# Three feed-forward layers by seven products instead of eight in 31 inner blocks, with one buffer pool and some low parts made by DMA

## The chip, the cores and the metric

The kernel runs on one core of one Trainium2 chip. The metric is the device time of one execution in microseconds (us).

## What is computed

Two layers of a diffusion trunk over 256 latent tokens (`L`) and 256 context tokens (`C`), 1024 features each. Every layer is a half-step SwiGLU feed forward, a token mixer (retention in layer 0, 2-D neighbourhood attention in layer 1), and another half-step feed forward; each is preceded by an RMS norm and a shift and scale taken from a modulation vector (`SiLU(c)` times a large matrix).

```python
def swiglu(x, w_in, w_out):
    a, b = jnp.split(x @ w_in, 2, axis=-1)
    return (jax.nn.silu(a) * b) @ w_out
# x: 256 + 256 tokens x 1024, w_in: 1024 x 5632, w_out: 2816 x 1024, four times
```

The fourth feed forward only has the latent tokens.

## The kernel before

Everything is kept in single precision on TensorE by splitting each operand into a high part (a rounding copy to the `float32r` format, made by ScalarE) and a low part (operand minus high part, made by VectorE). A product is then three matmuls: high weight by high input, high weight by low input, low weight by high input (`acc3`, L614). Every matmul is issued at L259, every VectorE, ScalarE and GpSimd operation at L151, every load at L166, so the rows are told apart by tile names: `raw` (a weight as loaded), `whi` and `wlo` (its parts), `slot` (activations and their parts), `t` (scratch), `pair` and `one` (PSUM: two banks, or one bank, of 512 words per partition), `acc` and `mraw` (the modulation).

A feed forward has 22 inner units of 128 hidden features. For one unit (`ffn`, the loop over `t`), two outputs of 128 features (a and b) are accumulated over eight blocks of 128 inputs, three matmuls each, with all 512 tokens as columns: 48 matmuls, the two outputs in the two banks of a `pair`. `gated_part` (L750) then makes silu(a) on ScalarE, the product on VectorE, and its high and low part. After 11 inner units the eight output blocks of `wout` are accumulated over those 11, and `residual` (L853) adds each to the stream `h`; then the other 11 units and eight blocks follow. In the last two output blocks the two streams are done apart, 256 columns at a time, so that the next norm can start.

The order is written by a planner: each emitted instruction advances an estimated clock of its engine (`account`, L131, with a fixed cost and a rate for each engine), and `advance` (L228), called after every matmul, emits pending VectorE and ScalarE steps when their estimated time has come. Steps wait in lists: `later` (evacuations, through `at`), `soon` (weight parts), and `bg`, the modulation of later sublayers, which VectorE computes by multiply-adds of 128x512 in the background, one step each `BG_EVERY` us of planned TensorE time. `mcol` (L445) hands out modulation columns that must be there by then. Weights are loaded in the order of `plan`: two raw buffers, three buffers for each part. Each engine executes its instructions in the order in which they were emitted; buffers and PSUM banks are guarded by semaphores.

## Time and profile before

| | |
|---|---|
| runs | 1949.91, 1951.44, 1952.09 us, median 1951.44 |
| the profiled execution | 1952.25 us, of which the span from first to last instruction is 1950.2 us |
| TensorE clock granted, mean | 0.994 of full speed |
| HBM | 276.11 MB read, 142 GB/s over the span |
| inner units of the three feed forwards with both streams | 66, at 48 matmuls of 512 columns |

Busy times of an engine are sums of its instructions' records. Matmuls are pipelined, so a matmul's recorded duration is longer than its distance to the next one, and a TensorE that is busy all the time can still be made to do less work. The distance from start to start is what one matmul costs in a dense stretch.

### The profile page before, as it was taken

The numbers are of one execution on the slowest core, as the hardware profiler recorded it, in microseconds if no ns is written. First come the engines' busy times: TensorE is split into PE (matmuls) and PEld (weight loads), VectorE is DVE, ScalarE is ACT, GpSimd is POOL, SyncE is SP. The second block draws the span as 40 slices with busy tenths as digits, with TensorE's granted clock in tenths as the row PEclk, the third lists the DMA queues.
The fourth block names the chain that finished last, engine by engine and source line by source line (L and its number), as shares of the span: only waits on it lengthen the run. The fifth ranks groups of instructions, "written<-read, shape, count | busy, mean of one in ns | idle before, by whom it ended". The sixth has DMA issues, their size and how long they took to land.

```text
span 1950.2 us, 26148 instructions
## 1 busy us (share of the span) xinstructions
PE 1924.2 (99%) x10458; PEld 1661.8 (85%) x10458; DVE 1352.0 (69%) x2402; ACT 687.9 (35%) x1035; POOL 73.0 (4%) x108
## 2 busy tenths in 40 slices
PE   7999999999999999999999999999999999999998
PEld 4888888898888888888888889888888899989998
DVE  5576666678788888876666676767632588887665
ACT  5422232333323232342222223322222366665443
POOL 1000000010000000100000000000000101100000
PEclk8999999999999999999999999999999999999999
DMA  7334534434434434234353343555433345544553
GB/s 287 141 137 129 187 130 136 156 119 151 142 133 141 147 130 142 86 130 149 125 179 132 140 139 98 194 189 200 162 101 82 110 119 113 98 115 167 194 176 114
DMA packets 70090, 278.85 MB, mean 143 GB/s; under 512 B 23632, under 2 KB 23888, under 8 KB 52304
## 3 DMA queue, kind: packets, MB, share of 16 engines
q1 hardware_dynamic: 69968, 277.18, 43.5%
q8 instruction: 82, 1.34, 0.3%
q14 instruction: 40, 0.33, 0.0%
HBM read 276.11 MB, written 1.05 MB: 142 GB/s over the span
## 4 chain that ended last, share of the span: by engine, by line
PE 94%; DVE 3%; ACT 2%; DMA 1%; issue 0%; SPq 0%; DVEq 0%; ACTq 0%
PE pair L259 61%; PE one L259 32%; DVE slot L151 1%; PE one L265 1%; DMA slot<-in_wmod 1%; DVE t L151 1%; ACT slot L151 1%; DVE wlo L151 1%; ACT whi L151 1%; DVE few L151 0%; DMA raw<-in_nv 0%; ACT t L151 0%; DVE h L151 0%; PE pair L265 0%; SPq L166 0%
## 5 line engine op out<-in xcount | busy, mean ns | idle before, releaser
L259 PE MATMUL pair<-slot,whi 128*128 128x512 f32 (+2 forms) x4000 | 1039.1, 351 | 6.8 <-ACT slot L151 4.7
L259 PEld LDWEIGHTS pair<-slot,whi 128*128 128x128 f32 x4000 | 696.4, 190 | 104.3 <-ACT slot L151 5.4
L259 PE MATMUL pair<-slot,wlo 128*128 128x512 f32 (+2 forms) x2000 | 682.5, 350 | 0.1
L259 PE MATMUL one<-slot,whi 128*128 128x512 f32 (+1 forms) x1860 | 481.4, 347 | 0.0
L151 DVE TENSOR_TENSOR wlo<-raw,whi 128x1024 fp32r<-128x1024 f32 (+1 forms) x400 | 436.4, 1122 | 38.5 <-ACT whi L151 37.7
L151 ACT CAST whi<-raw 128x1024 fp32r<-128x1024 f32 (+1 forms) x400 | 365.0, 959 | 225.3 <-PE one L259 138.6
L259 PEld LDWEIGHTS pair<-slot,wlo 128*128 128x128 f32 x2000 | 372.9, 190 | 48.8 <-DVE wlo L151 0.4
L259 PEld LDWEIGHTS one<-slot,whi 128*128 128x128 f32 x1860 | 325.9, 189 | 43.4
L259 PE MATMUL one<-slot,wlo 128*128 128x512 f32 (+1 forms) x930 | 323.1, 347 | 0.0
L151 DVE SCALAR_TENSOR_TENSOR acc<-mraw,sT,acc 128x512 f32<-128x512 f32 x392 | 279.2, 750 | 17.1 <-DMA mraw<-in_wmod 15.9
L151 ACT ACTIVATE t<-pair 128x512 f32<-128x512 f32 x66 | 39.4, 597 | 442.9 <-PE pair L259 442.9
L259 PEld LDWEIGHTS one<-slot,wlo 128*128 128x128 f32 x930 | 176.1, 189 | 21.8
L151 DVE TENSOR_TENSOR t<-pair,t 128x512 f32<-128x512 f32 x66 | 45.6, 692 | 204.2 <-ACT t L151 204.2
L151 DVE TENSOR_TENSOR slot<-t,slot 128x512 fp32r<-128x512 f32 (+2 forms) x144 | 88.1, 612 | 64.8 <-ACT slot L151 63.4
L151 ACT CAST slot<-t 128x512 fp32r<-128x512 f32 (+2 forms) x144 | 79.4, 552 | 122.1 <-DVE t L151 121.7
L151 DVE SCALAR_TENSOR_TENSOR h<-one,gate,h 128x256 f32<-128x256 f32 x112 | 49.6, 479 | 103.6 <-PE one L259 103.4
L151 POOL TENSOR_TENSOR t<-t,t 128x256 f32<-128x256 f32 x47 | 39.4, 850 | 1708.4 <-ACT t L151 1286.9
L259 PE MATMUL pair<-whi,slot 128*128 128x512 f32 (+1 forms) x384 | 98.5, 339 | 0.0
L259 PE MATMUL one<-slot,slot 128*128 128x512 f32 (+1 forms) x432 | 89.8, 348 | 1.3 <-DVE slot L151 1.0
L151 ACT ACTIVATE t<-h 128x256 f32<-128x256 f32 (+1 forms) x88 | 36.9, 434 | 142.8 <-DVE h L151 129.3
L259 PEld LDWEIGHTS one<-slot,slot 128*128 128x128 f32 x432 | 69.9, 189 | 10.8 <-DVE slot L151 1.4
L259 PEld LDWEIGHTS pair<-whi,slot 128*128 128x128 f32 x384 | 67.2, 189 | 7.5
(100 smaller groups left out, 1077.8 us busy)
## 6 DMA issues: line engine op xcount, KB each, us to landing
raw<-in_win SPq DMA_DIRECT2D x88, 1024.0 KB, 4.9
mraw<-in_wmod SPq DMA_DIRECT2D x128, 512.0 KB, 4.7
raw<-in_wout SPq DMA_DIRECT2D x64, 704.0 KB, 4.2
slot<-in_wmod SPq DMA_DIRECT2D x16, 512.0 KB, 10.3
raw<-in_rv SPq DMA_DIRECT2D x8, 1024.0 KB, 4.8
raw<-in_rg SPq DMA_DIRECT2D x8, 1024.0 KB, 4.9
raw<-in_ro SPq DMA_DIRECT2D x8, 1024.0 KB, 4.9
slot<-in_ex SPq DMA_DIRECT2D x8, 512.0 KB, 6.0
```

The lines of the kernel that those rows point to most:

```text
L151: getattr(self.real, op)(*args, **kw)
L259: nc.tensor.matmul(out, lhsT=lhsT, rhs=rhs, start=start, stop=stop)
L265: nc.tensor.transpose(out=out, in_=in_, identity=ident)
```

## The change

In 31 of the 66 units (7, 12 and 12 of the three feed forwards: `STANDARD` gives the first unit, `AMONG` the pattern) the product is arranged as a 2 by 2 block product: two outputs (a, b), two halves of the inputs (four blocks of 128 each), two token streams. Eight block products are replaced by seven with sums (Strassen's scheme in Winograd's form). Each of the seven has 4 blocks by 3 matmuls of 256 columns (`product`). The sums of the weight blocks are made on VectorE (`Seven`), the sums of the input blocks once for each feed forward (`operands`, not shown below: eight sums of 128x512 and four of 128x1024, and four pairs of parts of 128x1024), and the sums of the results when PSUM is read (`seven`). The low part of the b block of each such unit is not subtracted by VectorE: ScalarE writes minus the high part, and a DMA from GpSimd's queue reads the weight again from memory and adds it (`low_by_dma`). The same is done to half of every weight of the two mixers (`mixed`, 48 weights). Further: one pool of 40 buffers of 4 KB takes the place of three pools with the same room in all; weights are loaded in pieces of 512 KB; the 22 units are cut into three parts (8, 7, 7) in place of two, in all four feed forwards; the planner's fixed costs and rates are other ones; `BG_EVERY` is 0.9; a modulation column that isn't made when it is asked for is made there and then.

```diff
-HALF = NHC // 2
+PARTS = ((0, 8), (8, 15), (15, 22))
...
+SLOTS, RAWS, SPLITS = 40, 4, 12
+DMA_LOW = True
+MIXED = True
 BIG = 1e30
+STANDARD, AMONG = (8, 5, 5), (2, 3, 3)
...
-    slots = ctx.enter_context(tc.tile_pool(name="slots", bufs=24))
+    slots = ctx.enter_context(tc.tile_pool(name="slots", bufs=SLOTS))
...
-    V = Engine("dve", nc.vector, 0.06, 960.0)
-    A_ = Engine("act", nc.scalar, 0.09, 1200.0)
+    V = Engine("dve", nc.vector, 0.157, 960.0)
+    A_ = Engine("act", nc.scalar, 0.155, 1150.0)
...
+    def in_seven(f, t):
+        return f < 3 and t >= STANDARD[f] and (t - STANDARD[f]) % AMONG[f] < AMONG[f] - 1
+    def halves(src):
+        k = src.shape[1] // 2
+        return [src[:, i * k:(i + 1) * k, :] for i in range(2)]
+    def plan_ffn(f):
+        for p, (t0, t1) in enumerate(PARTS):
+            for t in range(t0, t1):
+                if in_seven(f, t):
+                    plan.append(("seven", [a["wrow"][f, t, r] for r in range(2)]))
+                else:
+                    plan.append(("plain", halves(a["win"][f, t])))
+            plan.extend(("plain", [a["wout"][f, n][:, t0:t1, :]]) for n in range(KC))
...
+        two = lambda *srcs: plan.extend((MIXED and "mixed" or "plain", halves(x)) for x in srcs)
...
-        account("pe", [lhsT, rhs], [out], n / 2400.0 * (1 if rhs.dtype == F32R and n >= 256 else 4) + 0.0025)
+        account("pe", [lhsT, rhs], [out], n / 2400.0 * (1 if rhs.dtype == F32R and n >= 256 else 4) + 0.0136)
...
+    def low_by_dma(lo, hi, src):
+        A_.activation(out=lo, in_=hi.bitcast(F32), func=AF.Copy, scale=-1.0)
+        nc.gpsimd.dma_start(out=lo.rearrange("p (k c) -> p k c", k=src.shape[1]), in_=src.bitcast(F32R), accum_op=ALU.add)
+        now["dma"] = max(now["dma"], now["act"])
+        account("dma", [], [lo], P * int(np.prod(src.shape[1:])) * 4 / 190e3)
+        ready[key(lo)] = (now["dma"] + 4.0, "dma")
...
+            if kind == "mixed" and i == 1:
+                def second(hi=hi, lo=lo, src=src, n=n):
+                    low_by_dma(lo[:, :n], hi[:, :n], src)
...
+            def low_b():
+                lo, hi = part_tile(), self.tiles["b", 0]
+                self.tiles["b", 1] = lo
+                low_by_dma(lo, hi, srcs[1])
...
+            steps = [(0.0, cast("b", rb), rb, 1), (0.8, DMA_LOW and low_b or low("b", rb), rb, 1), (1.5, p1, ra, 0),
+                     (2.2, p1_hi, ra, 1), (2.4, add(ra[:, f0], ra[:, f0], rb[:, f0]), ra, 0),
+                     (3.2, add(rb[:, f0], lambda: box["p1"], rb[:, f0]), rb, 0), (4.0, p1_lo, rb, 0),
+                     (4.6, add(rb[:, f1], rb[:, f0], rb[:, f1]), rb, 0), (5.2, cast("p", rb), rb, 1),
+                     (6.0, low("p", rb, True), rb, 1), (7.0, cast("a", ra), ra, 1), (8.0, low("a", ra, True), ra, 1)]
...
+            tile, last, half = {"b0": ("b", 1, 0), "b1": ("b", 1, 1), "p1": ("p1", 6, None), "a1": ("a", 11, 1),
+                                "p3": ("a", 11, 0), "p2": ("p", 9, 0), "p4": ("p", 9, 1)}[name]
+            force(self.no, last)
+            return [(t if half is None else t[:, half * 512:half * 512 + 512]).rearrange("p (k c) -> p k c", k=4)
+                    for t in (self.tiles[tile, 0], self.tiles[tile, 1])]
...
+    def released(n):
+        state["parts"] -= n
+        pump()
...
-            if raws and state["split"] - state["retired"] < SPLITS:
+            if raws and (not split_tiles if raws[0][0] == "seven" else
+                         state["parts"] + 2 * len(raws[0][1]) <= state["limit"] and not any(x[6] for x in soon)):
...
-    BG_EVERY = 2.2
+    BG_EVERY = 0.9
...
-        assert all((l, v, (c0 + k) // 4) in made for k in range(kk.start, kk.stop))
+        while not all((l, v, (c0 + k) // 4) in made for k in range(kk.start, kk.stop)):
+            if due:
+                mod_sum(*due.pop(0)[1])
+            else:
+                next(bg, None)
...
+    def product(w, name, x7, out):
+        wh, wl = w.part(name)
+        for k in range(4):
+            xh, xl = x7[name](k)
+            mm(out, lhsT=wh[:, k, :], rhs=xh, start=k == 0, stop=False)
+            mm(out, lhsT=wh[:, k, :], rhs=xl, start=False, stop=False)
+            mm(out, lhsT=wl[:, k, :], rhs=xh, start=False, stop=k == 3)
+    def seven(t, dst, x7):
+        w = weight()
+        p, b_, u_, a_, m1 = pair(), t512(), t512(), t512(), t256()
+        both = lambda x: x.rearrange("p (s t) -> p s t", t=S)
+        twice = lambda x: x.unsqueeze(1).broadcast_to([P, 2, S])
+        then = lambda step, on=None, us=0.2: at(us, L, t, step, on)
+        product(w, "b0", x7, p[:, 0, 0:S])
+        then(lambda: A_.copy(out=m1, in_=p[:, 0, 0:S]))
+        product(w, "b1", x7, p[:, 1, 0:S])
+        released(2)
+        product(w, "p2", x7, p[:, 1, S:T2])
+        then(lambda: V.tensor_tensor(out=both(b_), in0=both(p[:, 1, :]), in1=twice(m1), op=ALU.add))
+        q = pair()
+        product(w, "p3", x7, q[:, 1, S:T2])
+        product(w, "p1", x7, q[:, 1, 0:S])
+        released(1)
+        then(lambda: V.tensor_tensor(out=both(u_), in0=both(q[:, 1, :]), in1=twice(b_[:, S:T2]), op=ALU.add))
+        product(w, "p4", x7, q[:, 0, S:T2])
+        released(2)
+        then(lambda: V.tensor_tensor(out=b_[:, S:T2], in0=q[:, 0, S:T2], in1=u_[:, 0:S], op=ALU.add))
+        product(w, "a1", x7, q[:, 0, 0:S])
+        released(2)
+        then(lambda: V.tensor_tensor(out=both(a_), in0=q[:, :, 0:S], in1=twice(u_[:, S:T2]), op=ALU.add))
+        then(lambda: A_.activation(out=a_, in_=a_, func=AF.Silu, scale=-1.0), a_, 0.0)
+        then(lambda: V.tensor_tensor(out=b_, in0=b_, in1=a_, op=ALU.mult), a_, 0.0)
+        then(lambda: A_.copy(out=dst[:, 0, :], in_=b_), b_, 0.0)
+        then(lambda: V.tensor_tensor(out=dst[:, 1, :], in0=b_, in1=dst[:, 0, :].bitcast(F32), op=ALU.subtract), dst, 0.0)
...
-            for t in range(len(gts), HALF):
+            for t in range(len(gts), size):
+                if t0 + t == standard:
+                    x7 = made_operands()
+                    state["limit"] = SPLITS
+                if in_seven(2 * l + which, t0 + t):
+                    gts.append(slot([P, 2, 512], F32R))
+                    seven(t, gts[t], x7)
+                    continue
+                if not raw and t0 + t == standard - 3 and standard < PARTS[0][1]:
+                    made_operands = operands(xt)
+                if t0 + t == standard - 3 and standard == PARTS[0][1]:
+                    state["limit"] = SPLITS - 4
...
+            if raw or t1 > standard:
+                need(L, size - 2)
             for w, ps in zip(ws, pss):
-                acc3_part(ps[:, every], terms(w, every, range(HALF - 1)), True, False)
-            if raw:
-                need(L, HALF - 1)
+                acc3_part(ps[:, every], terms(w, every, range(size - 1)), True, False)
+            if raw or t1 > standard:
```

## Rows read from the trace of the kernel before

**Rows 1.** The page's first part: engine, busy us (share), instructions.

```profile
PE 1924.2 (99%) x10458; PEld 1661.8 (85%) x10458; DVE 1352.0 (69%) x2402; ACT 687.9 (35%) x1035; POOL 73.0 (4%) x108
```

**Rows 2.** The page's chain that ended last, by engine.

```profile
PE 94%; DVE 3%; ACT 2%; DMA 1%; issue 0%; SPq 0%; DVEq 0%; ACTq 0%
```

**Rows 3.** Windows: stretch, us, then busy us and count of each engine, clock, DMA.

```profile
175.00:295.00 120.00, 120.00 (x533) 99.38 (x532) 80.67 (x131) 28.82 (x36) 0.00 (x0) 1.00 0.45 155
...
440.00:835.00 395.00, 393.95 (x1927) 333.15 (x1926) 327.75 (x605) 128.67 (x171) 7.49 (x10) 1.00 0.39 132
...
1560.00:1755.00 195.00, 189.97 (x1383) 177.70 (x1384) 163.36 (x331) 124.56 (x231) 25.00 (x32) 1.00 0.51 111
```

**Rows 4.** Timeline of an inner unit, 512 columns: start, us, engine, operation.

```profile
1033.55 0.62 PE L259 MATMUL pair<-slot,whi 128*128 128x512 f32 x2
...
1043.78 0.62 PE L259 MATMUL pair<-slot,whi 128*128 128x512 f32 x2
```

**Rows 5.** Timeline of the last output blocks, 256 columns.

```profile
1175.53 0.40 PE L259 MATMUL one<-slot,whi 128*128 128x256 f32 x2
...
1184.89 0.40 PE L259 MATMUL one<-slot,whi 128*128 128x256 f32 x2
```

**Rows 6.** Groups by form, VectorE: out, in, count, busy us, mean ns.

```profile
L151 DVE TENSOR_TENSOR wlo<-raw,whi 128x1024 fp32r<-128x1024 f32 x272 | 324.3, 1222 | 21.5 <-ACT whi L151 21.0
L151 DVE SCALAR_TENSOR_TENSOR acc<-mraw,sT,acc 128x512 f32<-128x512 f32 x392 | 279.2, 750 | 17.1 <-DMA mraw<-in_wmod 15.9
L151 DVE TENSOR_TENSOR wlo<-raw,whi 128x704 fp32r<-128x704 f32 x128 | 112.1, 910 | 17.1 <-ACT whi L151 16.7
L151 DVE TENSOR_TENSOR slot<-t,slot 128x512 fp32r<-128x512 f32 x98 | 67.8, 692 | 56.8 <-ACT slot L151 56.3
L151 DVE SCALAR_TENSOR_TENSOR h<-one,gate,h 128x256 f32<-128x256 f32 x112 | 49.6, 479 | 103.6 <-PE one L259 103.4
...
L151 DVE TENSOR_TENSOR t<-one,t 64x256 f32<-64x256 f32 x16 | 6.7, 420 | 0.6 <-ACT t L151 0.2
L151 DVE TENSOR_TENSOR t<-t,t 128x512 f32<-128x512 f32 x8 | 5.5, 693 | 0.3
```

**Rows 7.** Groups by form, ScalarE.

```profile
L151 ACT CAST whi<-raw 128x1024 fp32r<-128x1024 f32 x272 | 272.0, 1045 | 117.7 <-PE one L259 102.2 <-DMA raw<-in_win 7.2 <-issue 4.7
...
L151 ACT CAST slot<-t 128x512 fp32r<-128x512 f32 x98 | 60.8, 621 | 96.1 <-DVE t L151 96.0
...
L151 ACT ACTIVATE t<-pair 128x512 f32<-128x512 f32 x66 | 39.4, 597 | 442.9 <-PE pair L259 442.9
...
L151 ACT COPY slot<-one 128x256 f32<-128x256 f32 x1 | 0.4, 373 | 5.9 <-PE one L259 5.9
```

**Rows 8.** DMA queues and issues: KB each, median us to landing.

```profile
q1 hardware_dynamic: 69968, 277.18, 43.5%
...
mraw<-in_wmod SPq DMA_DIRECT2D x128, 512.0 KB, 4.7
...
slot<-in_wmod SPq DMA_DIRECT2D x16, 512.0 KB, 10.3
```

**Rows 9.** Groups by form, TensorE: a matmul of 256 columns.

```profile
L259 PE MATMUL one<-slot,wlo 128*128 128x256 f32 x372 | 105.7, 284 | 0.0
```

**Rows 10.** Timeline around the end of an inner unit.

```profile
1020.15 0.39 PE L259 MATMUL pair<-slot,wlo 128*128 128x512 f32 x1
...
1020.58 0.60 ACT L151 ACTIVATE t<-pair 128x512 f32<-128x512 f32 x1 [9.10 <-PE pair L259]
```

**Rows 11.** Timeline of VectorE releasing TensorE in the norm.

```profile
36.54 0.48 DVE L151 TENSOR_SCALAR t<-con,few 128x128 f32<-128x128 f32 x2
...
36.88 0.71 PE L259 MATMUL one<-t,con 128*128 128x128 f32 x4 [1.94 <-DVE t L151]
```

**Rows 12.** Chain of waits in the neighbourhood attention, shares by line.

```profile
by line: PE pair L259 45.5%; PE one L259 12.5%; ACT slot L151 5.8%; PE one L265 5.7%; ACT whi L151 5.6%; DVE slot L151 5.4%; DVE wlo L151 5.1%; DVE t L151 4.7%; issue 2.9%; DMA raw<-in_nv 2.5%; DVE h L151 1.3%; ACT t L151 1.3%; DVE few L151
```

More of the change, by code (lines that the diff above doesn't have):

```diff
@@ new lines, in plan_all @@
+    def plan_all():
+        two = lambda *srcs: plan.extend((MIXED and "mixed" or "plain", halves(x)) for x in srcs)
+        plan_ffn(0)
+        for hd in range(H_RET):
+            two(a["rq"][hd], a["rk"][hd], a["rv"][hd, 0], a["rv"][hd, 1])
+            if hd:
+                two(a["ro"][hd - 1, 0], a["ro"][hd - 1, 1])
+            two(a["rg"][hd, 0], a["rg"][hd, 1])
+        two(a["ro"][H_RET - 1, 0], a["ro"][H_RET - 1, 1])
+        plan_ffn(1)
+        plan_ffn(2)
+        for g in range(4):
+            two(a["nq"][g], a["nk"][g], a["nv"][g])
+        two(*(a["no"][n] for n in range(4)))
+        plan_ffn(3)
@@ L232, in advance @@
         go(later[L])
-        while soon and not state["tight"] and soon[0][0] <= now["pe"] and ready_at(soon[0][5]) <= now["pe"] + 0.3 and free("dve", 0.5):
+        while soon and not state["tight"] and soon[0][0] <= now["pe"] and ready_at(soon[0][5]) <= now["pe"] + 0.3 and free("dve", 0.5) and state["parts"] + soon[0][6] <= SPLITS:
             soon.pop(0)[2]()
@@ L277, in prep, with landed @@
+    def landed(n):
+        state["raw"] -= n
+        pump()
     def prep():
[L278 removed]
+        kind, units, srcs = raws.pop(0)
         tile_no = state["split"]
         state["split"] += 1
[L281 to L296 removed]
@@ L722, in cols, with operands, add, whole @@
         return slice(ss[0] * S, ss[0] * S + S * len(ss))
+    def operands(xt):
+        q = lambda kh, s, part: [xt[2 * kh + i][part][:, :, s * S:s * S + S] for i in range(2)]
+        sums_, parts_ = {}, {}
+        flat = lambda t: t.rearrange("p a b -> p (a b)")
+        def add(step, on, e="dve"):
+            at(0.0, "parts", 0, step, on, 0.4, e)
+        def whole(kh, s):
+            def step(i):
+                if i == 0:
+                    sums_[kh, s] = slot([P, 4, S])
+                hi, lo = (q(kh, s, part)[i] for part in range(2))
+                V.tensor_tensor(out=sums_[kh, s][:, 2 * i:2 * i + 2, :], in0=hi.bitcast(F32), in1=lo.bitcast(F32), op=ALU.add)
+            for i in range(2):
+                add(lambda i=i: step(i), xt[2 * kh + i][1])
+        def combine(name, dst, op, *srcs):
+            def step():
+                x, y = (flat(parts_[n] if isinstance(n, int) else sums_[n]) for n in srcs)
+                out = flat(sums_[dst])
+                if op == "minus":
+                    V.tensor_tensor(out=out, in0=x, in1=y, op=ALU.subtract)
+                else:
+                    V.scalar_tensor_tensor(out=out, in0=x, scalar=-1.0, in1=y, op0=ALU.mult, op1=ALU.subtract)
+                parts_[name] = sums_[dst]
+            add(step, xt[3][1])
+        def two(name):
+            box = []
+            def hi():
+                box.extend(slots2([P, 4, S]))
+                A_.copy(out=flat(box[0]), in_=flat(parts_[name]))
+            def lo():
+                V.tensor_tensor(out=flat(box[1]), in0=flat(parts_[name]), in1=flat(box[0]).bitcast(F32), op=ALU.subtract)
+                made_[name] = box
+            add(hi, xt[3][1], "act")
+            add(lo, xt[3][1])
+        made_ = {}
+        whole(0, L)
+        whole(0, C)
+        whole(1, C)
+        combine(1, (0, L), "minus", (0, L), (0, C))
+        two(1)
+        combine(3, (0, C), "minus", (1, C), (0, C))
+        combine(2, (1, C), "opposite", 1, (1, C))
+        two(2)
+        whole(1, L)
+        two(3)
+        combine(4, (1, L), "opposite", 2, (1, L))
+        two(4)
+        y = lambda n: lambda k: (made_[n][0][:, k, :], made_[n][1][:, k, :])
+        x = lambda kh, s: lambda k: tuple(xt[2 * kh + k // 2][part][:, k % 2, s * S:s * S + S] for part in range(2))
+        def rest():
+            need("parts", 0)
+            return {"b0": x(0, L), "b1": x(1, L), "p4": x(1, C), "p1": y(1), "p2": y(2), "p3": y(3), "a1": y(4)}
+        return rest
@@ L725, in ffn @@
     def ffn(l, i, xt, streams, g, done, ahead=None, raw=None, between=None, third=(16.0, 16.0)):
         every = cols(streams)
+        which, standard = i, NHC if raw else STANDARD[2 * l + i]
         wide = slice(0, WIDE) if raw else every
@@ L757, in ffn @@
         raw_ps = {}
-        for hf in range(2):
+        for hf, (t0, t1) in enumerate(PARTS):
             gts = []
+            size, final = t1 - t0, hf == len(PARTS) - 1
             if hf == 0:
@@ L829, in ffn @@
                         ps = one()
[L830 removed]
+                        acc3(ps[:, xc], terms(w, xc, range(size)))
                         if s == streams[-1]:
```

159 lines of the change are left out of this document (98 added, 61 removed).

## The prediction

> **What bounds the kernel now.** I read the page's first part and its chain first. TensorE is busy 1924.2 of 1950.2 us [rows 1] and 94% of the chain is TensorE [rows 2]: apart from about 26 us (the start, the end, the neighbourhood attention) the time is a stream of matmuls. Windows say the same by stage: in a feed forward TensorE has 120.00 of 120 us with VectorE at 80.67, in retention 393.95 of 395 with VectorE at 327.75, in the neighbourhood attention 189.97 of 195 with VectorE at 163.36 [rows 3]. So a change pays by what it takes out of TensorE's stream, and VectorE, two thirds full in the feed forwards, decides whether it gets it.
>
> A busy TensorE says nothing of the price of a matmul; the distance from start to start does. In an inner unit 45 matmuls of 512 columns lie between the two rows of [rows 4]: (1043.78 - 1033.55) / 45 = 0.2273 us. In the last output blocks 78 of 256 columns lie between those of [rows 5]: (1184.89 - 1175.53) / 78 = 0.1200 us. Every matmul there has its own weight load, so a weight load hides behind 256 columns too. Two of 256 cost 0.2400, 13 ns more than one of 512.
>
> **The seven products.** A unit is 48 x 0.2273 = 10.91 us; a seven is 7 x 4 x 3 = 84 matmuls, 84 x 0.1200 = 10.08 us. 31 times 0.83: **-25.8 us**. This is two thirds of the eighth that Strassen's scheme promises; the rest goes to the 13 ns.
>
> **What VectorE gets.** In a seven: p1, three sums and the low part of p1, each 128x512 at 0.693 or 0.692, and two low parts of 128x1024 at 1.222, make 5.9 us; the evacuation has five instructions of 128x512 (about 0.69 each) and one of 128x256 (0.42, the 256-column form read from PSUM), 3.9 us [rows 6]. Together 9.8 of its 10.08 us. A standard unit has 2 x 1.222 + 2 x 0.692 = 3.8. Two sevens and one standard unit, the pattern of the second and third feed forward, need 23.4 of 31.1 us: 75%. The first feed forward alternates, 13.6 of 21.0. The background steps (0.750 each) have to live in what is left, and BG_EVERY 0.9 lets them run faster wherever VectorE is free, above all in the eight or five standard units ahead. Over the kernel: 31 x 6.0 = +184; `operands` 8 x 0.69 + 8 x 1.222 = 15.3, three times, +46; the third part of each feed forward 16 more residuals (8 in the last) at 0.479, +27; 48 low parts of mixers by DMA -59; output weights in 96 pieces of up to 1024 in place of 128 of 704 (0.910), about -6. Sum +192 on 1352: 79% of the span. It fits as a total; cover is missing only inside the runs of sevens. Background steps that are late for `mcol` would now be made on the spot at 0.750 each with TensorE waiting; the standard units ahead and retention give them room, so I count 0. ScalarE gets about 3.1 us more in a seven by [rows 7] (four copies of 1.045 and one of 0.621 for two of 1.045, and 0.373 for m1), in all some +160 on 687.9: hidden.
>
> **The read in the middle of a bank.** `seven` puts p4 into columns 256 to 511 of q's first bank, then a1 into columns 0 to 255 of the same bank. The step that adds p4 is due 0.2 us after p4 in planned time, so it is emitted after the second matmul of a1 (2 x 0.12). Everywhere else in the code, before and in `seven`, a bank is read only after all that goes into it was issued (m1, b_ and u_ read other banks than the one being written; the last output blocks take a whole bank for 256 columns). If the guard works by bank, a1's third matmul waits for VectorE here. The price from rows: a 256-column matmul is recorded at 0.284 and the next is due after 0.120, so 0.164 is exposed [rows 9]; the end of a matmul to the start of its reader is 1020.58 - (1020.15 + 0.39) = 0.04 [rows 10]; the read is 0.420; from the first of two VectorE instructions (36.54 + 0.24) to TensorE's start at 36.88 is 0.10 [rows 11]. Sum 0.72 us, the floor. Queued behind it on TensorE is everything. Above: one low part of 1.222 that stands ahead of the read on VectorE, 1.95. Below: nothing, if only overlapping columns are guarded. No row shows such a read, so I choose between them: I take the floor, since p4's 1.44 us leave room for u_ and one more 0.69 instruction, and each stall gives VectorE 0.7 us that the planner didn't count on. 31 x 0.72 = **+22.3**, nearly the whole gain.
>
> The Trainium skill (PSUM — Partial Sum Buffer, section on bank collisions) says that TensorE writing and VectorE reading one bank at once is an error even at different columns, and that software has to guard by bank. By this rule the stall exists; without it the sum would be 22.3 us lower. No run here shows it yet.
>
> **Low parts by DMA.** 79 of them (31 and 48), 512 KB each, 41 MB more from memory on 276: the queue's share of 43.5% has room [rows 8]. No row shows an adding DMA. Bounds by plain ones of 512 KB: 4.7 us to landing, 10.3 in the queue at the start. A seven's parts are begun when the unit ahead begins; two ScalarE instructions of 1.045 and 4.7 us land at 6.8 of its 10.1 us: hidden, 0. With 10.3 they land at 12.4, 1.6 us late with a stall counted in, and the low matmul of b0 is the third one, so nothing covers it. I take the near end, as the transfer is like `mraw` in size and in a running kernel.
>
> **Parts, pool, planner.** Last output blocks: 11 to 7 blocks by halves, (24 x 0.2273 - 48 x 0.1200) = -0.3 in three feed forwards, **-0.9**. The first two output blocks still give 2 x 6 x 3 x 0.2273 = 8.2 us of cover to the last unit's evacuation (some 4 us). Two loads of 512 KB for one of 1024 KB double the issues on SyncE, which isn't on the chain. In the neighbourhood attention 5.1% of the chain is `wlo` and 5.6% `whi` [rows 12], some 10 us each of 195; 16 low halves leave VectorE, and the planner's costs fit its rows better. TensorE lacks 5 us there, which bounds the gain; a late low part could cost as much as it saves. I take **-2**, between 0 and -5.
>
> **Sum.** 1952.25 (the profiled execution) - 25.8 + 22.3 - 0.9 - 2 = 1945.9. The median of the runs is 0.8 lower than that execution: **1945 us**. Against 1951.44 that is -0.33%; 0.2%, 3.9 us, is about what a measurement of this kernel can tell from no change.
>
> **Rivals.**
> - *Gain eaten at the floor* (forecast, 0.46): its own range is 1943 (the attention gives 4 in place of 2) to 1957 (a stall of 1.1). Faster by over 0.2% as long as the stall stays under 0.80: 0.27; within: 0.17; slower: 0.02.
> - *No stall* (0.22): guards by columns, or the read lands in a gap. 1945 - 22.3 = 1923, with 3 to 5 us lost to a full VectorE 1927. For it: nothing in the trace of before stalls on PSUM. Against: the care in the code to keep reads and writes in different banks.
> - *VectorE stands in the way* (0.22, slower): the same read, but behind other VectorE work, because a run of sevens leaves VectorE 3% free before background steps. From a mean stall of 0.93 on the change loses; with half of the reads behind one 1.222 instruction, 0.72 + 0.61 = 1.33, 1945 + 31 x 0.61 = 1964; with all, 1983. For it: the 9.8 of 10.08. Against: each stall is itself 0.72 of free VectorE.
> - *Low parts late* (0.10, slower): landing over 8.7 us from issue. At 10.3: 31 x 1.6 = +50, 1995.
>
> Slower 0.02 + 0.20 + 0.10 = 0.32, within 0.2% 0.17 + 0.02 = 0.19, faster 0.27 + 0.22 = 0.49. The range takes in no stall, and the read behind half to two thirds of low parts: 1922 to 1974, with some 0.08 left out below and 0.12 above.
>
> **What would show it.** Right: matmuls of 256 columns in the inner units at 0.120 apart, and 31 idle times of TensorE of about 0.72 us in a1, each ended by VectorE's `t<-pair,t` of 128x256; VectorE near 1540 us in all; HBM read near 317 MB. Wrong: TensorE idle at b0's third matmul, ended by a DMA (late low parts); distances over 0.12 between matmuls (weight loads that no longer hide); VectorE's idle share near zero in a run of sevens; no idle time in a1 at all.

## The result, and the profile after

The change makes the kernel slower: 2076.1 us (median of 4 runs, 2075.0 to 2080.0) against 1951.7 for the kernel before beside it, a ratio of 1.064 with a 95% interval of 1.062 to 1.066. The forecast was 1945 with a range to 1974. So 124 us have to be explained, where the forecast had stalls of 22.

First the page of the changed kernel, its first part: engine, busy us (share), instructions.

```profile
span 2078.2 us, 29555 instructions
PE 1947.1 (94%) x11502; PEld 1716.9 (83%) x11502; DVE 1532.5 (74%) x2705; ACT 836.6 (40%) x1187; POOL 144.0 (7%) x187
HBM read 317.52 MB, written 1.05 MB: 153 GB/s over the span
```

Against [rows 1], TensorE's idle time has grown from 26 us to 131. VectorE's total and the bytes are those of the forecast (1544 us, 317 MB), so the work was counted right. What was wrong is who waits for it. The waits of TensorE, by what ended them (us in total, times, longest):

```profile
PE pair L281 <- DVE t L161: 46.7, 62, 2.2
PE pair L281 <- ACT t L161: 23.8, 21, 4.7
PE pair L281 <- ACT slot L161: 10.2, 6, 2.4
PE one L281 <- DVE small L161: 6.5, 2, 4.3
PE one L281 <- DMA wp<-in_rv: 5.8, 1, 5.8
```

The forecast named 31 waits for VectorE's `t`, one in each seven. There are 62, twice 31, and 21 more for ScalarE's. Where they stand is read in the timeline of TensorE over two sevens in a row in the second feed forward (start, us, operation, count; in brackets the idle time ahead and what ended it):

```profile
1015.43 1.83 PE L281 MATMUL pair<-slot,wp 128*128 128x256 f32 x14
1017.72 6.02 PE L281 MATMUL pair<-slot,wp 128*128 128x256 f32 x48 [0.46 <-ACT t L161]
1024.67 1.70 PE L281 MATMUL pair<-slot,wp 128*128 128x256 f32 x12 [0.93 <-DVE t L161]
1026.88 8.89 PE L281 MATMUL pair<-slot,wp 128*128 128x256 f32 x72 [0.52 <-DVE t L161]
1036.56 1.69 PE L281 MATMUL pair<-slot,wp 128*128 128x256 f32 x12 [0.78 <-DVE t L161]
1038.76 2.61 PE L281 MATMUL pair<-slot,wp 128*128 128x256 f32 x15 [0.52 <-DVE t L161]
```

Count the matmuls, 12 to a product. 14 are b0 and two of b1: TensorE waits at b1's third matmul. 48 are the other 10 of b1, then p2, p3, p1 and two of p4: the next wait is at p4's third. 12 more end at two of a1: a wait at a1's third. The second seven has the last two of the three. The pace between the waits is the forecast's: 72 matmuls in 8.89 us, the last one recorded at 0.29, make (8.89 - 0.29) / 71 = 0.121 [rows 5].

What a wait costs is the distance between the starts less 0.12 for each matmul. At b1: 17.72 - 15.43 - 14 x 0.12 = 0.61. At p4: 24.67 - 17.72 - 48 x 0.12 = 1.19, and 1.04 in the second seven. At a1: 26.88 - 24.67 - 12 x 0.12 = 0.77, and 0.76. Only this last was in the forecast, at 0.72. What TensorE waits for at p4 and at a1 is seen in VectorE's timeline beside it:

```profile
1023.93 0.69 DVE L161 TENSOR_TENSOR t<-pair,t 128x512 f32<-128x512 f32 x1
1026.40 0.42 DVE L161 TENSOR_TENSOR t<-pair,t 128x256 f32<-128x256 f32 x1 [1.19 <-PE pair L281]
```

The first is u_, which reads the second bank of q. It ends at 1024.62, and at 1024.67 TensorE goes on with p4, which it writes into q's *first* bank. So the wait is not for the bank that is read. It looks as if the whole tile `pair`, two banks, were guarded as one.

The time of each stage, in all the kernels of this study, from the last `t<-t,t` of a norm on GpSimd (its additions of squares) to that of the next; what comes after the last one is 10 to 12 us in each. "FF" are the four feed forwards, "ret" retention, "nat" the neighbourhood attention. An indented kernel is the nearest one above that is indented less, with one more change. Stages are those of one profiled execution, which can lie beside the median: 6.3 us above it in "and m1 later", 3.9 in "changed", within 3 us in the others.

```
                                  FF 1    ret   FF 2   FF 3    nat   FF 4   median
before                           411.1  416.4  362.0  365.6  193.1  190.3   1951.7
changed                          436.0  431.9  398.4  400.1  206.1  195.1   2076.1
p4 in p                          422.5  431.0  376.0  377.3  204.7  197.3   2019.7
 and m1 later                    417.5  430.5  375.9  381.2  206.9  197.6   2015.9
  a quarter of the steps         416.4  459.3  376.7  364.7  195.0  192.3   2019.3
  a quarter of steps and loads   413.6  432.9  364.7  367.7  197.7  192.3   1980.5
  low DMA moved to FF 1 to 3     434.1  418.3  383.0  398.9  235.3  193.0   2077.4
  b's low part on VectorE        417.4  434.4  367.2  395.6  267.7  199.7   2095.9
  low parts on GpSimd            418.4  438.3  381.2  387.6  200.0  192.3   2031.4
   two sums on GpSimd            425.4  449.5  390.4  400.0  198.5  192.2   2066.3
changed, mixers by VectorE       433.5  419.7  393.0  400.4  219.4  199.8   2075.6
no sevens                        416.7  432.6  369.1  367.6  194.2  192.3   1984.3
 and mixers by VectorE           415.4  419.5  366.5  371.0  193.3  193.2   1971.3
  two parts                      411.9  416.2  367.0  365.2  193.2  191.6   1958.6
  old costs                      421.5  426.9  365.7  365.5  189.5  191.3   1973.6
  both                           413.2  421.9  363.2  363.2  190.0  189.9   1956.6
   12 sevens in FF 3             413.2  424.3  363.2  360.7  190.1  189.9   1955.2
  both, new costs in ret         411.7  416.6  365.6  363.2  190.1  189.9   1952.0
   10 sevens in FF 3             413.2  416.6  365.6  356.8  190.1  189.9   1945.9
```

Every stage of the changed kernel is longer, those without a seven too: retention by 15.5 us, the neighbourhood attention by 13.0, the last feed forward by 4.8.

### The profile page after: what moved, and what is told of

It reads as the page before. It is cut to its first block, busy times and chain, and to the rows that moved or that the text cites. A ratio compares the mean times of both kernels' runs of the same rounds, so it can differ in the third digit from the quotient of the medians.

```text
span 2078.2 us, 29555 instructions
## 1 busy us (share of the span) xinstructions
PE 1947.1 (94%) x11502; PEld 1716.9 (83%) x11502; DVE 1532.5 (74%) x2705; ACT 836.6 (40%) x1187; POOL 144.0 (7%) x187
## 5 line engine op out<-in xcount | busy, mean ns | idle before, releaser
L281 PE MATMUL pair<-slot,wp 128*128 128x256 f32 (+2 forms) x7116 | 1157.5, 322 | 93.5 <-DVE t L161 46.7
L281 PEld LDWEIGHTS pair<-slot,wp 128*128 128x128 f32 x7116 | 1029.9, 194 | 202.6 <-DVE t L161 59.8
L281 PE MATMUL one<-slot,wp 128*128 128x512 f32 (+1 forms) x2718 | 525.8, 354 | 2.8 <-DMA wp<-in_ro 2.8
L281 PEld LDWEIGHTS one<-slot,wp 128*128 128x128 f32 x2718 | 447.1, 190 | 71.5 <-ACT wp L161 3.2
L161 ACT CAST wp<-raw 128x1024 fp32r<-128x1024 f32 (+1 forms) x399 | 393.0, 1027 | 161.1 <-DVE raw L161 80.0
L161 DVE TENSOR_TENSOR wp<-raw,wp 128x1024 fp32r<-128x1024 f32 (+1 forms) x320 | 377.0, 1199 | 38.1 <-ACT wp L161 37.5
L161 DVE SCALAR_TENSOR_TENSOR acc<-mraw,sT,acc 128x512 f32<-128x512 f32 x392 | 284.9, 762 | 18.7 <-DMA mraw<-in_wmod 17.8
L161 DVE TENSOR_TENSOR t<-pair,t 128x512 f32<-128x512 f32 (+1 forms) x159 | 101.6, 639 | 151.7 <-PE pair L281 84.3
L281 PE MATMUL pair<-wp,slot 128*128 128x512 f32 (+1 forms) x576 | 104.5, 338 | 0.7 <-DVE slot L161 0.7
L281 PEld LDWEIGHTS pair<-wp,slot 128*128 128x128 f32 x576 | 89.7, 189 | 12.3 <-DVE slot L161 1.1
L161 ACT ACTIVATE wp<-wp 128x1024 fp32r<-128x1024 f32 x79 | 83.7, 1060 | 7.7 <-PE one L281 5.7
```

What stands on the lines that cost most here:

```text
L161: getattr(self.real, op)(*args, **kw)
L281: nc.tensor.matmul(out, lhsT=lhsT, rhs=rhs, start=start, stop=stop)
```

## The experiments

### Is it the tile, or a VectorE that is too full?

The only edit is the place of p4: its columns in p in place of q.

```diff
-        product(w, "p4", x7, q[:, 0, S:T2])
+        product(w, "p4", x7, p[:, 0, S:T2])
...
-        then(lambda: V.tensor_tensor(out=b_[:, S:T2], in0=q[:, 0, S:T2], in1=u_[:, 0:S], op=ALU.add))
+        then(lambda: V.tensor_tensor(out=b_[:, S:T2], in0=p[:, 0, S:T2], in1=u_[:, 0:S], op=ALU.add))
```

> Only p4's place changes: columns 256 to 511 of p's first bank in place of q's. Same instructions, same work on every engine. Theory (the guard works over the whole two-bank tile `pair`: u_ is read from q's second bank while p4 is written to its first, and TensorE waits; b_ is read from it while a1 is written): both reads now leave q or p alone while the other is written, the 62 waits of TensorE for VectorE's `t` (46.7 us in the changed kernel) go, and with the exposed end of a matmul (some 0.16 each time) that is 50 to 55 us: 2076 - 53 = 2023. The stall at b1 (m1, 21 waits for ScalarE, 23.8 us) stays. Rival (VectorE is too full in a seven, 9.8 of 10.08 us, and the waits are only where its lateness shows): the waits move to the next place that needs VectorE (the buffers of `pair`, operands, low parts), and the time stays within 10 us of 2076.

2019.7 us (2019.4 to 2021.2): 56.4 less, where 53 was expected. The waits of TensorE in this kernel:

```profile
PE pair L281 <- ACT t L161: 24.0, 21, 4.7
PE pair L281 <- DVE t L161: 2.1, 5, 0.5
```

57 of 62 waits for VectorE have gone with 44.6 us, and VectorE did the same work (1530.2 us busy). At b1, where m1 is still read from p's first bank while b1 goes into its second, the 21 waits for ScalarE stand as before. The rival falls: the two stalls come from where the results stand. The Trainium skill (PSUM — Partial Sum Buffer, section on bank collisions) asks that two engines be kept apart by bank. By that alone p4's first bank and u_'s second need no wait. Here they had one of 1.0 to 1.2 us, and it went when the tile was another one: this program keeps them apart by the tile, which is coarser.

The same for m1, with its copy after p2:

```diff
-        then(lambda: A_.copy(out=m1, in_=p[:, 0, 0:S]))
         product(w, "b1", x7, p[:, 1, 0:S])
         released(2)
         product(w, "p2", x7, p[:, 1, S:T2])
+        then(lambda: A_.copy(out=m1, in_=p[:, 0, 0:S]))
...
-        then(lambda: V.tensor_tensor(out=both(b_), in0=both(p[:, 1, :]), in1=twice(m1), op=ALU.add))
+        then(lambda: V.tensor_tensor(out=both(b_), in0=both(p[:, 1, :]), in1=twice(m1), op=ALU.add), m1)
```

> As the kernel with p4 in p, and ScalarE's copy m1 is emitted after p2 instead of during b1, the sum b_ when m1 is planned to be there. So no bank of a tile is read while another one of it is written. Theory (guard over the whole tile): the 19 waits of about 0.7 for ScalarE inside sevens go too (14 us and 19 x 0.16 of exposed matmuls, 17 us), the two of 4.9 us at the first seven of the second and third feed forward need not: 2023 - 17 = 2006. Rival (ScalarE or VectorE late): m1 only moves, u_ comes later, and nothing or a loss of a few us follows against the kernel with p4 in p.

2015.9 us (2013.6 to 2022.2): 3.8 less, not 17, and as the two kernels' runs overlap, a gain is not shown. The waits for ScalarE's `t` are gone, but others have come:

```profile
PE pair L281 <- DMA wp<-in_wrow: 10.2, 5, 2.8
PE pair L281 <- ACT wp L161: 6.0, 3, 2.8
```

So here the rival's figure is right: where the waits at b1 go, low and high parts of the weights come late in their place, as if the stalls had given them time.

### How much lies outside the sevens?

```diff
-STANDARD, AMONG = (8, 5, 5), (2, 3, 3)
+STANDARD, AMONG = (99, 99, 99), (2, 3, 3)
```

> No inner unit is made by seven products; the one pool, three parts, mixed low parts by DMA and the planner's new costs stay. Theory: the sevens' stalls go (46.7 + 23.8 us and 83 x 0.16 exposed = 84) and so does the gain of fewer matmuls (+25.8): 2076 - 84 + 26 = 2018, so that some 66 us of the loss of 125 lie outside the sevens. Rival (the rest of the change costs nothing, and all of the loss comes from sevens, directly or by what they take from VectorE): 1952.

1984.3 us. Both miss. 32.6 us of the loss have nothing to do with sevens, half of them in retention (table). And the sevens cost 91.8 net, 34 more than the stalls less the gain come to. In the kernel with m1 later they still cost 31.6: 7 and 14 in the second and third feed forward, and 13 and 5 in the last two stages, which have none (by stages, of an execution 6.3 us above its median).

### The mixers' low parts

```diff
-MIXED = True
+MIXED = False
```

> The 48 low parts of the mixers' weights go back to VectorE; all else stays. Theory (the low part by DMA comes too late where the unit has few matmuls ahead of it: waits of 5.95, 2.94, 2.3 in retention and about 7 in the neighbourhood attention, each followed by matmuls at half the clock): most of the 15.8 + 13.0 us that these two stages have lost comes back, 2076 - 20 = 2056, and no wait of TensorE for a DMA into `wp` is left in them. Rival (the DMA waits stand where VectorE would have been late as well, 48 x 1.222 = 59 us more of its work): 2076 or up to 10 above.

2075.6 us, no change: the rival's figure, but the stages tell more. Retention gives 12.2 us back, the neighbourhood attention takes 13.3. In retention of the changed kernel the timelines of GpSimd and of TensorE show one low part: issued at 475.47, it lands 8.5 us later, and TensorE has stood for it since 478.3.

```profile
475.47 0.86 POOL L306 DMA_DIRECT2D wp<-in_rv  x1 [20.37 <-ACT wp L161]
```

```profile
465.62 12.66 PE L281 MATMUL one<-wp,slot 128*128 128x512 f32 x55
484.07 11.86 PE L281 MATMUL one<-wp,slot 128*128 128x512 f32 x41 [5.79 <-DMA wp<-in_rv]
```

With mixers by VectorE there is no such wait. What the neighbourhood attention waits for instead, in TensorE's timeline of that kernel:

```profile
1847.61 0.60 PE L281 MATMUL one<-small,con 128*128 128x16 f32 x2 [10.91 <-DVE small L161]
1859.57 0.58 PE L281 MATMUL one<-small,con 128*128 128x16 f32 x2 [11.36 <-DVE small L161]
```

`small` is the sum of a modulation block. The gate needs it, the background has not made it, and `mcol` has it made on the spot. The steps themselves, `acc`, show how late the background is: count, min/median/max ns, first and last start. The first line is of the kernel before, the second of the changed one:

```profile
L151 DVE SCALAR_TENSOR_TENSOR acc<-mraw,sT,acc x392: 719/747/1239, 86.7 to 1394.2; 128x512 f32<-128x512 f32 x196
```

```profile
L161 DVE SCALAR_TENSOR_TENSOR acc<-mraw,sT,acc x392: 718/747/2743, 90.1 to 1925.0; 128x512 f32<-128x512 f32 x196
```

Before, the last step starts at 1394, in the middle of the third feed forward. Now at 1925, in the last. Without sevens there is no such lack (the last step starts at 1286, in the third feed forward), and so the other half can be seen alone, with both switches:

> No sevens (1984), and the mixers' low parts on VectorE too. With mixers by VectorE alone the whole time did not move, since retention gave 12 us back and late modulation took 23 us in the neighbourhood attention. Theory (both are so: low parts by DMA cost retention 12 us, and the modulation was late only because sevens had filled VectorE): without sevens the 12 us stay won, no wait for `small` of over 2 us: 1970 to 1972. Rival (what retention gains is lost elsewhere again): 1980 to 1988.

1971.3 us, 13.0 less than without sevens alone; retention 419.5. The low parts by DMA cost the mixers 13 us, and the modulation was late only with sevens.

### How much is the full VectorE?

The background modulation is cut to a quarter: first only its steps (the first edit), then its loads as well (the second). The base is the kernel with m1 later; both leave out work, so the modulation that they compute is another one.

```diff
-                for k in range(2):
+                for k in range(2 if q == 0 else 0):
```

```diff
-    quarters = [(l, b, q) for l, b, _ in bg_list for q in range(4)]
+    quarters = [(l, b, q) for l, b, _ in bg_list for q in range(1)]
...
-            for q in range(4):
+            for q in range(1):
```

> As the kernel with p4 in p and m1 later (2016), but three quarters of the background modulation's accumulations are left out (112 of 448 steps stay, so the modulation is another one than the reference's): some 336 x 0.75 = 250 us less on VectorE, nothing else changes. Theory (what is left of the loss in the feed forwards with sevens, and in the two last stages, is a full VectorE: the background steps, none of which stood in the last two stages before, now reach into them with 33 of 448): the neighbourhood attention falls from 207 to 194 and the last feed forward from 198 to 192, as in the kernel without sevens, and the second and third feed forward from 376 and 381 to 365 or less: 1963 to 1985. Rival (low parts by DMA and casts on ScalarE come late whatever VectorE does): the second and third feed forward stay at 372 or more, only the last two stages gain: about 1998.

2019.3 us: neither. The third feed forward, the neighbourhood attention and the last feed forward come out as the theory says (364.7, 195.0, 192.3), but the second feed forward stays and retention loses 29 us. The experiment had a flaw, which VectorE's timeline there shows: with the steps left out, the loads come four times as close, and VectorE's queue stands behind one of them. The read for TensorE at 750.29 is behind it.

```profile
749.88 0.49 DVE L161 TENSOR_SCALAR acc<-mraw,sT 128x512 f32<-128x512 f32 x1 [10.07 <-DMA mraw<-in_wmod]
750.29 0.69 DVE L161 TENSOR_TENSOR slot<-pair,slot 128x512 fp32r<-128x512 f32 x1
```

> As the kernel with p4 in p and m1 later (2016), with only the first quarter of the background modulation: three quarters of its loads and of its steps are left out, so the modulation is another than the reference's. In the run that left out the steps alone, four times the loads came in the same time, and VectorE stood 10 us behind one of them with a read for TensorE queued behind it. Theory (a full VectorE costs the third feed forward, the neighbourhood attention and the last stage some 34 us, as that run showed in 365, 195 and 192): the same three values, and retention back at 430 or less: 1972 to 1985. Rival (the loss in retention came from fewer steps themselves, by another order): retention stays near 459, 2010 or more.

1980.5 us, 35.4 less than the kernel with m1 later, inside the theory's range; the second feed forward falls too, by 11. So with the two-bank stalls gone, the VectorE time that the modulation wants is worth 35 us at most (its loads are left out with it). And even then the second and third feed forward, 364.7 and 367.7, are no shorter than before with 12 sevens in each.

### Three other ways for the low parts

The base is again the kernel with m1 later. First 32 of retention's to VectorE and 29 of standard inner units to the DMA:

```diff
-                    plan.append(("plain", halves(a["win"][f, t])))
+                    plan.append(("mixed" if f < 3 and t > 1 else "plain", halves(a["win"][f, t])))
...
-        two = lambda *srcs: plan.extend((MIXED and "mixed" or "plain", halves(x)) for x in srcs)
+        two = lambda *srcs: plan.extend(("plain", halves(x)) for x in srcs)
...
+        two = lambda *srcs: plan.extend(("mixed", halves(x)) for x in srcs)
         for g in range(4):
```

> As the kernel with p4 in p and m1 later (2016), but the 32 low parts by DMA of retention go back to VectorE (+39 us) and 29 low parts of standard inner units, from the third unit on in the first three feed forwards, go to the DMA instead (-35 us), so VectorE's total stays. A standard unit has 10.9 us of matmuls, retention's units far less. Theory (a low part by DMA costs where fewer us of matmuls stand ahead of it than the 8 to 11 us that it takes to land): retention from 430 to 418, the feed forwards unchanged: 2004. Rival (GpSimd's queue or memory is what is short): the DMA waits move into the feed forwards, 2016 or more.

2077.4 us. Retention gives its 12 us back (418.3), but all other stages except the last one lose. TensorE's waits:

```profile
PE pair L282 <- DMA wp<-in_wrow: 15.5, 6, 5.0
PE pair L282 <- DMA wp<-in_win: 12.6, 7, 4.1
```

For the 29 of standard units TensorE waited 7 times: 10.9 us of matmuls ahead don't always cover such a low part either. The neighbourhood attention, whose low parts still come by DMA, loses 28 us: TensorE's waits for them there grew from 8.1 to 18.7 us. The rest wasn't followed further.

Then b's low part in each seven to VectorE:

```diff
-DMA_LOW = True
+DMA_LOW = False
```

> As the kernel with p4 in p and m1 later (2016), but the low part of b in a seven is made by VectorE (31 x 1.222 = +38 us) and not by ScalarE and DMA. Theory (the low part by DMA is one of the things that are late in a seven: 10.2 us in 5 waits for it): these waits go, VectorE's own waits in the sevens grow, and the modulation reaches further into the last stages: 2010 to 2030, no clear gain. Rival (the DMA is the limit of what is left, VectorE is not): 2000 or less.

2095.9 us. The second feed forward gains 8.7 us (367.2), so its low parts by DMA were late. But with 38 us more on VectorE the modulation is later still: TensorE waits 54.5 us in 6 times for `small`, 12.4 of them at once in the third feed forward and 34.1 in the neighbourhood attention. No clear gain, as the theory had it, and a loss far beyond its 2030.

GpSimd is busy for 7% of the span. So the 79 low parts go there, as one subtraction, and in a second kernel two of a seven's sums as well:

```diff
-                low_by_dma(lo, hi, srcs[1])
+                G_.tensor_tensor(out=lo, in0=rb, in1=hi.bitcast(F32), op=ALU.subtract)
...
-                V.tensor_tensor(out=box["p1"], in0=ra[:, f0], in1=ra[:, f1], op=ALU.add)
+                G_.tensor_tensor(out=box["p1"], in0=ra[:, f0], in1=ra[:, f1], op=ALU.add)
```

> As the kernel with p4 in p and m1 later (2016), but all 79 low parts that went by ScalarE (x -1) and DMA are one subtraction of 128x1024 on GpSimd, from the raw tile in the buffer. By its row of 128x256 (0.85 to 0.90 us) that is an estimated 3 to 3.6 us each, against 1.06 + 8.5 us; ScalarE loses 79 x 1.06 = 84 us. Theory (these low parts are late by their way, not by VectorE's load): retention falls from 430 to about 418, the second feed forward from 376 to 368 as with b's low part on VectorE, the third by as much, the neighbourhood attention by some 5: 2016 - 12 - 8 - 8 - 5 = 1983. Rival (GpSimd and VectorE slow each other at the buffer, so that VectorE's subtractions and GpSimd's take much longer): 2010 or more.

2031.4 us, 15.5 more: the rival. The subtraction is no longer than thought (the first line, GpSimd's, 2.57 us), but VectorE's steps beside it are (the second line):

```profile
L161 POOL TENSOR_TENSOR wp<-raw,wp 128x1024 fp32r<-128x1024 f32 x79 | 202.5, 2565 | 1272.0 <-ACT wp L161 932.4 <-DMA raw<-in_win 131.6 <-PE one L281 63.7
L161 DVE SCALAR_TENSOR_TENSOR acc<-mraw,sT,acc 128x512 f32<-128x512 f32 x392 | 330.9, 881 | 13.5 <-DMA mraw<-in_wmod 12.5
```

881 ns in place of 762 in the kernel with m1 later, and VectorE is busy 1631 us in place of 1530.

> As the kernel with low parts on GpSimd, and of each seven two of the four sums over weights (p1, and the sum into a's tile) go to GpSimd too: 31 x 2 x 0.69 = 43 us off VectorE. Theory (a full VectorE pushes the background modulation into the last stages): fewer of the 33 late steps remain there, the third feed forward, the neighbourhood attention and the last one gain together 10 us or more on the kernel with low parts on GpSimd. Rival (what is left in the sevens is a chain of dependent steps, and a sum that takes 1.5 to 1.8 us in place of 0.69 makes it longer): the feed forwards with sevens lose by more than that.

2066.3 us, 35 more again: the rival. The neighbourhood attention gains 1.5 us, the feed forwards with sevens lose 7 to 12, retention 11.

### What is left without sevens: 20 us

Two parts as before (output weights in pieces of 6 and 5 blocks), the planner's old costs (VectorE's fixed one is shown; ScalarE's and a matmul's go back too), and both:

```diff
-PARTS = ((0, 8), (8, 15), (15, 22))
+PARTS = ((0, 11), (11, 22))
...
-    V = Engine("dve", nc.vector, 0.157, 960.0)
+    V = Engine("dve", nc.vector, 0.06, 960.0)
```

> The kernel without sevens and with mixers by VectorE (1971.3, still 19.6 above the kernel before), and the inner units in two parts of 11 as before (output weights in pieces of 6 and 5 blocks). Theory (the third part costs: one more change from inner units to output blocks in each feed forward, where the last inner units are waited for, and 24 more residuals): each of the four feed forwards gives back 3 to 4 us, 1955 to 1960. Rival (the planner's costs, which say that VectorE's and ScalarE's steps take longer than the planner thought before, let background and low parts go later): no change, 1969 to 1973.

> The kernel without sevens and with mixers by VectorE (1971.3), three parts, and the planner's costs of the kernel before (VectorE 0.06 us fixed, ScalarE 0.09, 2.5 ns on a matmul). Theory (the third part costs): no change, 1969 to 1973. Rival (the planner's new costs): 1955 to 1960.

> Both at once: without sevens, mixers by VectorE, two parts, the planner's old costs. What is left of the change is the one pool of buffers, weights loaded in halves and their limits. If these cost nothing: 1950 to 1954. If they do: what stays above 1952 is theirs.

1958.6, 1973.6 and 1956.6 us. The third part costs 12.8 us, though not evenly, as expected, but in the first and third feed forward and in retention behind the first. A part of it is seen where the next stage begins (behind the first feed forward; three parts, then two):

```profile
419.82 7.45 PE L281 MATMUL pair<-slot,wp 128*128 128x256 f32 x38 [2.12 <-ACT slot L161]
```

```profile
417.03 5.02 PE L281 MATMUL pair<-slot,wp 128*128 128x256 f32 x38 [0.34 <-DVE slot L161]
```

TensorE waits 2.12 us in place of 0.34, and the same 38 matmuls take 2.4 us longer; behind the second and third feed forward the waits are 2.14 and 3.35, with two parts 0.34 and 0.65. An estimate of the reason, which no run tests: the last output blocks now sum over 7 blocks in place of 11, so each half covers 4 x 3 x 0.12 = 1.4 us less of the next norm.

The planner's old costs move the sum little (2.2 us more with three parts, 2.0 less with two). In the stages they show: with the old ones retention is 5.7 us longer (421.9 against 416.2), all behind it but the last 11 us 10.7 us shorter. So a kernel was tried with the new costs in retention alone (below): 1952.0, the time of the kernel before. What is left of the change (the one pool, the halves and their limits, and `BG_EVERY`) costs 5 us with the old costs, where retention is 5.5 longer than before (421.9 against 416.4), and nothing that can be measured with the new ones there. Why retention needs them is not shown.

### Does a seven pay at all?

All that had hurt is taken away: two parts, low parts by VectorE, p4 in p, m1 later, and sevens only in the third feed forward, in whose middle the modulation ended before.

> As that kernel, with 12 sevens in the third feed forward alone (p4 in p, m1 later, all low parts on VectorE): before, VectorE had room there, since the background modulation ends in it. Theory (a seven pays once no tile is read while its other bank is written, no low part comes by DMA and VectorE isn't full): 12 x 0.83 = 10 us less, 1 to 3 us lost at the first seven, so 7 to 9 us below the kernel with both. Rival (sevens lose anyway, by the casts and operands ahead of the first one): no gain or a loss against it.

1955.2 us (1953.8 to 1955.9), 1.4 below the kernel without them (1953.8 to 1958.3, so the runs overlap); the stage itself 2.5 shorter. The forecast of 7 to 9 fails. TensorE's waits in that stage:

```profile
PE pair L281 <- ACT wp L161: 2.8, 1, 2.8
PE pair L281 <- DVE wp L161: 0.9, 1, 0.9
PE pair L281 <- DVE t L161: 0.2, 1, 0.2
```

The first two are both at the first seven, where ScalarE and VectorE still make the last operand. So the operands are begun five units ahead in place of three, and the first seven is unit 7.

```diff
-                if not raw and t0 + t == standard - 3 and standard < PARTS[0][1]:
+                if not raw and t0 + t == standard - 5 and standard < PARTS[0][1]:
...
+            planner(0.0136, 0.157, 0.155, 1150.0)
             retention(xt, GateLater(lambda: gate(0, 1, BOTH, 1.0)), done, *mixer)
+            planner(0.0025, 0.06, 0.09, 1200.0)
```

> As the kernel with sevens in the third feed forward alone (1955.2), with two changes. The planner's new costs hold during retention only: retention was 5.7 us shorter with them (416.2 against 421.9), the stages behind it shorter with the old ones. And the operands are begun five units ahead of the first seven in place of three, the first seven is unit 7 in place of 5 (10 sevens): TensorE stood 2.8 + 0.9 us at the first one, behind the last operand's cast on ScalarE. Theory: 1955.2 - 5.7 - 3.7 + 2 x 0.83 = 1947.5, below the kernel before (1951.6). Rival (the waits move: VectorE and ScalarE are as late at unit 7, and retention's 5.7 come back at its end): 1953 to 1956.

> The same with no seven at all: two parts, the planner's old costs, the new ones in retention only. Theory: 1956.6 - 5.7 = 1951, the time of the kernel before, and 10 sevens without a late start are worth 3 to 6 us against it (10 x 0.83 = 8.3, less what the stalls for low parts and the operands took before). Rival: 1955 or more, and no difference to the kernel with ten sevens.

1945.9 us (1944.7 to 1946.5) with ten sevens, 1952.0 without. Against the kernel before the ratio of the first is 0.9971 (0.9959 to 0.9983): it is 0.29% faster. The view of waits shows none of TensorE's in the third feed forward, which takes 6.4 us less than without sevens. A window over it (stretch, us, then busy us and count of each engine, clock, DMA) shows it full, with VectorE at 62%:

```profile
1195.00:1552.00 357.00, 356.54 (x2126) 318.67 (x2125) 220.88 (x329) 129.30 (x187) 7.43 (x11) 1.00 0.33 100
```

## Why the prediction was wrong, step by step

- **The read in the middle of a bank.** The stall at a1 came nearly as worked out, 0.76 to 0.77 against 0.72, but one term of the sum is off, one is missing, and they partly cancel. VectorE's read ends at 1026.82 and TensorE starts at 1026.88: 0.06, where the forecast took 0.10 from two instructions that overlap [rows 11]. And 0.16 + 0.04 + 0.42 + 0.06 leave 0.1 of the distance for which the sum has no term. The step that failed is the clause that "m1, b_ and u_ read other banks than the one being written" and so cost nothing. They read other banks of the same tile, and the wait covers the tile. In the two sevens shown p4 costs 1.0 to 1.2 us and b1 0.6 in the first; p4 and a1 together are 56.4 us (p4 in p), where the forecast had 22.3. The rival with no stall at all is out, and "guards by columns" with it.
- **The seven products.** The pace is 0.121 against 0.120. A seven was to save 0.83 us; ten saved 6.1 to 6.4, 0.61 to 0.64 each, once nothing stood in their way. In the changed kernel the other terms are several times that.
- **What VectorE gets.** The total was right (1532 against 1544). The step that failed is "the standard units ahead and retention give them room, so I count 0" for the modulation. The background had to give way and moved into stages that had none, 35 us at most. This was no rival of the forecast, whose VectorE rival spoke of the read alone.
- **Low parts by DMA.** In the sevens of the changed kernel they were hidden, as forecast, but with the stalls gone TensorE waits 10.2 us for them. The mixers' 48 were the miss: the forecast weighed the sevens' cover of 10 us and took -2 for the neighbourhood attention, without the same sum for units with far less cover. Without sevens they cost 13.0 us.
- **Parts and planner.** Counted at -0.9 for the last output blocks, with cover worked out for the last unit's evacuation and not for the next norm; the third part costs 12.8 and the planner's costs, behind retention, 6.6 (1958.6 to 1952.0).

These prices (56.4 + 3.8 + 35.4 + 13.0 + 12.8 + 6.6 = 128.0), measured on different kernels and 3.8 of them not clear of noise, need not add up to 124.4. With the sevens' own gain (31 x 0.62 = 19) some 16 us stay without a name; the late starts at the first sevens (4.7 us of waiting in each of two feed forwards) are part of them, the rest stays open. One share runs through these prices: the mean granted clock is 0.980 in the changed kernel and 0.994 before. Over the spans, 0.020 x 2078.2 less 0.006 x 1950.2 makes 30 us: an estimate, at most, of what a slower TensorE after its waits has cost. The forecast had no term for it. How many sevens pay in the second feed forward, where VectorE has the modulation to do, wasn't tried.

## What to carry to other kernels

Ask not only which bank an engine reads while TensorE writes, but which tile: results that are read early go into another tile than the one being written. Background work that an edit displaces has a price where it lands: follow it to the stage that needs it last, and ask who is forced to wait there. A faster inner loop also takes away the cover of all that was hidden behind it, so its operands have to be begun earlier, or the next late thing takes the gain.

## What the runs showed of the hardware

- GpSimd and VectorE got in each other's way. In the kernel with low parts on GpSimd, the 38 of the 392 `acc` steps whose time overlaps a GpSimd subtraction have a mean of 1.98 us, the other 354 one of 0.763, that of all of them in the kernel with m1 later (0.762). The Trainium skill (SBUF — State Buffer, section on the two separate sides) says that the two engines share a pair of ports under an exclusive lock, held for a whole instruction. A few long steps among unchanged ones agree with that.
- A longer wait cost more than itself. After the 4.74 us at the first seven of the second feed forward, 48 matmuls took 7.38 us, where the 48 at 1017.72 above took 6.02, and the granted clock from 920 to 960 us was 0.87 (the level of 2.4 GHz before and after, part of it at 1.2); after the 5.79 us for `in_rv` the stretch from 480 to 520 us had 0.91. TensorE's timeline and windows of the changed kernel:

```profile
932.99 7.38 PE L281 MATMUL pair<-slot,wp 128*128 128x256 f32 x48 [4.74 <-ACT t L161]
```

```profile
880.00:920.00 40.00, 38.64 (x215) 33.58 (x214) 28.23 (x41) 16.58 (x24) 0.00 (x0) 1.00 0.09 27
920.00:960.00 40.00, 31.45 (x195) 29.22 (x194) 25.19 (x33) 15.21 (x20) 1.75 (x2) 0.87 0.44 109
```

- An adding DMA of 512 KB took 5.6 us to land in the sevens (median of 31), little more than the plain load of a seven's weights (5.2), but 8.5 where TensorE waited for one in retention.
